# Low parts off GpSimd between the output projection and the early wide products, and kept weight parts at the head of the second half

## The chip, the cores and the metric

The kernel runs on one core of one Trainium2 chip. The metric is device time in microseconds (us). Five engines of the core matter here: TensorE does matrix products and transposes (PE in the profile, with its weight loads as PEld), VectorE (DVE) and ScalarE (ACT) do elementwise work, GpSimd (POOL) does elementwise work too, and SyncE (SP) issues the transfers. Each engine runs its own instructions in the order in which the program issued them, and waits at an instruction until what it reads has been written and the buffer that it writes has come free.

## The reference, cut to what matters

One layer of a hybrid streaming encoder is computed for two groups of tokens, 512 prompt tokens and 32 sample tokens, with a model width of 1024 and shared weights. The change touches the stretch from the output projection to the first products of the feed-forward part:

```python
mix = (g_a * y_a + g_b * y_b) @ w_o
x = layer_norm(ALPHA * x + (1 + g1) * mix, ln1_g, ln1_b)
h2 = layer_norm(x) * (1 + sc2) + sh2
gt, up = jnp.split(h2 @ w_gu, 2, axis=-1)
ffn = (jax.nn.silu(gt) * up) @ w_down
x = layer_norm(ALPHA * x + (1 + g2) * ffn, ln2_g, ln2_b)
```

`h2` therefore needs two layer norms of each token, one behind the other. `w_gu` is 1024 x 5632: 2816 columns for the gate and 2816 for `up`. One small edit lies far earlier, in the differential attention of the sample tokens.

## The kernel before

**Products in two parts.** Every large product is made of three float32r products: a factor is written as a high part (a rounded copy, `hi`, made by ScalarE) and a low part (`lo = raw - hi`), and the result is the sum of hi x hi, hi x low and low x hi. The weights are split while the kernel runs, in pieces of 128 rows x 8 x 128 columns (128x1024 elements). The activations are split too (`h2H`, `h2L` for `h2`).

**Units and the planner.** The kernel is a list of units that `stream` (L1258) walks through. A `Unit` (L1014) of the wide products has 24 matmuls for each half of the tokens (8 slices of the inner dimension, three products each). Half 0 is the tokens 0 to 255; half 1 is the tokens 256 to 511 and the 32 sample tokens, 288 columns. Before a unit runs, `prep` (L1287) has the next unit's weights split; `hi` and `lo` have two buffers each. Everything else (evacuations, norms, softmax) is written as generators that a planner, `Lane` (L467), steps in between the matmuls by its own model of time; its table `LATER` (L34) moves single steps by some microseconds. The planner runs when the program is built, so what it decides is the fixed order of instructions on each engine.

**Output projection.** Eight pieces of `w_o` are split by `split_to` (L2380), and `TokUnit`s accumulate one tile of 128 tokens and 512 columns at a time: first token tiles 0 and 1, then 2, then 3. `tok_end` multiplies by the gate (`z`), adds to `u_t` and takes statistics (`blk_st`).

**Two norms.** `norm_pair(p)` (L2280) starts two `norm_tile`s (L2228), the tiles 2p and 2p+1. A norm tile gets its reciprocal root from GpSimd (`rs`, L722 and L599), applies the norm, gain and bias to `u_t`, takes new statistics, gets a second root and lets ScalarE write `xn`. How gain and bias are applied is set by `MODE` (L2353). With 0 it is two VectorE instructions of 128x1024 (`scalar_tensor_tensor`). With 2, used for tile 2 alone, it is one on ScalarE, one on VectorE and one on GpSimd. Then four `quarter`s (L2288) transpose `xn` on TensorE (`ps_x`), scale and shift it (`h2t`, on ScalarE or VectorE by `ACT_MOD`), and `h2_parts` (L2266) writes `h2H` on ScalarE and `h2L` on VectorE, or on GpSimd for the quarters in `POOL_LO`. Pair 0 and `norm_rows` (the 32 sample tokens) come first; the tiles 2 and 3 feed half 1.

**Early wide products.** The first three column chunks of `w_gu` (`EARLY = 3`) run in halves: twelve units (chunk, column block, gate or up) with half 0, then the same twelve units with half 1, each with its weights split again, in the same order (`order`, L2510). Behind them each chunk runs with both halves. Chunk 0 comes through a ring of two raw buffers, chunks 1 and 2 lie in tiles of their own (`rawg`). The first unit of each half has `need_norm` (L2487): there the planner issues whatever is left of the norms of that half. For each unit, `g_evac` makes `th` from the gate product; `u_evac` (L2472) multiplies it with the `up` product and splits the result into `act` parts, the low part on VectorE, or on GpSimd for the entries of `ACT_POOL`.

**GpSimd's part.** `sub2` (L602) makes a low part in two pieces, 128x384 on GpSimd and 128x640 on VectorE. It is used by `split_to`, so for the pieces of `w_o` and for the splits of the early units.

**Attention.** `attention()` (L1590) begins with a copy of the sample tokens' queries (`q_s`, 128x128, L1594) out of the tile `qka`, on VectorE; the next step, `kH`, writes into the slot that this copy reads.

Of the kernel before, what the change touches and what calls it, by code (L numbers as in the profile page):

```python
# [9 lines left out]
F32 = mybir.dt.float32  # L10
F32R = mybir.dt.float32r
AF = mybir.ActivationFunctionType
# [230 lines left out]
    "norm_pair/1/28": 0.8,  # L243
# [4 lines left out]
    "norm_pair/1/32": -0.5,  # L248
# [11 lines left out]
    "norm_pair/1/5": 5,  # L260
# [14 lines left out]
    "norm_pair/1/9": -1,  # L275
    "norm_rows/0/0": 0.4,
# [6 lines left out]
    "norm_rows/0/8": 3,  # L283
# [3 lines left out]
    "norm_tile/0/5": -1,  # L287
# [94 lines left out]
    "tok_end.g/10/1": 0.4,  # L382
# [13 lines left out]
    "tok_end.g/7/0": 0.4,  # L396
    "tok_end.g/7/2": 0.8,
# [138 lines left out]
def trunk_kernel(ctx: ExitStack, tc: tile.TileContext, I: dict, O: list):  # L536
# [11 lines left out]
    lane = Lane()  # L548
# [24 lines left out]
    def act(out, in_, func, **kw):  # L573
        nc.scalar.activation(out=out, in_=in_, func=func, **kw)  # L574
        lane.op("act", out)
# [18 lines left out]
    def vtt(out, in0, in1, op):  # L594
        nc.vector.tensor_tensor(out=out, in0=in0, in1=in1, op=op)  # L595
        lane.op("dve", out)

    def gtt(out, in0, in1, op):
        nc.gpsimd.tensor_tensor(out=out, in0=in0, in1=in1, op=op)  # L599
# [21 lines left out]
    def vcopy(out, in_):  # L621
        nc.vector.tensor_copy(out=out, in_=in_)
        lane.op("dve", out, 0.8)
# [4 lines left out]
    ADD, SUB, MUL, MAX, MIN = ALU.add, ALU.subtract, ALU.mult, ALU.max, ALU.min  # L628
# [67 lines left out]
    for c in LOADS.split():  # L696
        n = int(c[1:])
# [211 lines left out]
    qk_holder = {}  # L909
# [422 lines left out]
    q_s = s3[:, 1824:1952].rearrange("p (h t) -> p h t", h=4)  # L1332
# [257 lines left out]
    def attention():  # L1590
# [3 lines left out]
        vcopy(q_s, qk_holder["q"][:, :, 512:544])  # L1594
# [463 lines left out]
    units = []  # L2058
# [96 lines left out]
    for br, (W, ev) in enumerate(((I["w_br_a"][0], br_a_evac), (I["w_br_b"][0], br_b_evac))):  # L2155
        for c in range(2):
            src = W[:, c * 512:(c + 1) * 512].rearrange("(k p) c -> p k c", p=128)
            ch = Chunk([(lambda r: r.rearrange("p (k c) -> p k c", k=4), src)])
            for j in range(4):
# [12 lines left out]
                u = Unit(ch, 0, 4, aH, aL, ev(4 * c + j), split=sp_br)  # L2172
# [55 lines left out]
    def norm_tile(tt):  # L2228
# [214 lines left out]
    h2Hk = lambda k: D_["h2H"](k)  # L2443
    h2Lk = lambda k: D_["h2L"](k)
# [42 lines left out]
    def need_norm(hf):  # L2487
        return lambda: lane.until(lambda: hf in norms and all(x[2] for x in norms[hf]))
# [5 lines left out]
    pairs = []  # L2494
    EARLY = 3
# [15 lines left out]
    for c, halves in order:  # L2511
        for j in range(2):
            n = 2 * c + j
            for g, ev in ((0, g_evac), (1, u_evac)):
                u = Unit(
                    pairs[c][g], 128 * j, 8, h2Hk, h2Lk, ev(n), halves=halves,
                    split=gu_split(c, j, g) if c < EARLY else None,
                )
                if (c, j, g) == (0, 0, 0):
                    u.need = need_norm(halves[0])  # L2520
                units.append(u)
        if c == 4:
            units.append(Call(lambda: state.update(gate=lane.add(gate_parts()))))
# [168 lines left out]
```

## Time and profile before

| | us |
|---|---|
| median of 3 runs | 940.01 (938.99 to 941.04) |
| the profiled execution | 941.38 |
| its span | 939.3 |
| TensorE busy | 900.0 (96%) |
| VectorE busy | 522.9 (56%) |
| ScalarE busy | 329.6 (35%) |
| GpSimd busy | 182.5 (19%) |

The span runs from the first to the last instruction of the profiled execution. TensorE is busy for 96% of it, so whole-span shares say little about a change in the order of the other engines: what counts is where TensorE stands still or runs at a lower clock. Of its 39 us of idle time, about 24 lie in the first 25 us and the last 27 us, which the change doesn't touch. The rest is short waits: some 7 us spread over the attention and the stages beside it, and some 8 us gathered between 506 and 546 us, which is the stage of this change. The prediction shows the lines of that stage.

### The profile page before, as it was taken

How to read it: one execution, taken by the hardware profiler on the slowest of the kernel's cores; microseconds unless marked ns; L12 is line 12 of the kernel's file. 1: busy time of each engine (PE TensorE's matmuls, PEld its weight loads, DVE VectorE, ACT ScalarE, POOL GpSimd, SP SyncE). 2: the span in 40 equal slices, each digit the busy share in tenths (PEclk: the TensorE clock that was granted, in tenths of full speed). 3: DMA queues.
4: the chain of work that ended last, by engine and by line, in shares of the span. 5: the costliest groups of instructions: out<-in, count | busy, mean ns of one | idle time of the engine just before them, and what ended most of it. 6: DMA issues, size and time to landing. Idle time of an engine off the chain costs nothing. (4 is left out here: it accounts for less than half of the span.)

```text
span 939.3 us, 16724 instructions
## 1 busy us (share of the span) xinstructions
PE 900.0 (96%) x6903; PEld 824.8 (88%) x6903; DVE 522.9 (56%) x1083; ACT 329.6 (35%) x653; POOL 182.5 (19%) x224
## 2 busy tenths in 40 slices
PE   4999999999999999999998999999999999999995
PEld 3899997988898989999886889999999999777885
DVE  4653559968445444457769865434564455224247
ACT  3343385556532333223403464322232332111110
POOL 3010145433300111103623745100000000000002
PEclk8999999999999999999998999999999999999998
DMA  9924244323343531216806002122332344613202
GB/s 291 342 85 117 83 127 135 102 90 97 132 157 113 185 107 48 95 51 231 263 1 227 32 18 90 47 85 92 126 113 87 124 135 158 238 51 133 90 24 95
DMA packets 89256, 113.05 MB, mean 120 GB/s; under 512 B 4432, under 2 KB 65204, under 8 KB 89180
## 3 DMA queue, kind: packets, MB, share of 16 engines
q1 hardware_dynamic: 88972, 111.92, 36.6%
q8 instruction: 54, 0.88, 0.4%
q14 instruction: 22, 0.18, 0.1%
q10 hardware_dynamic: 208, 0.07, 0.0%
HBM read 104.71 MB, written 7.26 MB: 119 GB/s over the span
## 5 line engine op out<-in xcount | busy, mean ns | idle before, releaser
L595 DVE TENSOR_TENSOR lo<-raw,hi 128x1024 fp32r<-128x1024 f32 (+2 forms) x100 | 113.3, 1133 | 155.3 <-ACT hi L574 154.6
L574 ACT ACTIVATE hi<-raw 128x1024 fp32r<-128x1024 f32 (+1 forms) x116 | 115.7, 997 | 189.5 <-PE dn L1075 78.0
L1043 PE MATMUL g<-h2La,hi 128*128 128x288 f32 (+1 forms) x352 | 102.3, 291 | 2.4 <-DVE h2La L595 1.8
L1043 PE MATMUL g<-h2Ha,lo 128*128 128x288 f32 (+1 forms) x352 | 101.8, 289 | 1.8 <-DVE lo L595 1.5
L1075 PE MATMUL dn<-hi,act 128*128 128x512 f32 (+1 forms) x356 | 103.5, 375 | 0.0
L1043 PE MATMUL g<-h2Hb,hi 128*128 128x288 f32 (+1 forms) x352 | 102.8, 292 | 0.0
L1043 PE MATMUL g<-h2Ha,hi 128*128 128x288 f32 (+1 forms) x352 | 102.3, 291 | 0.1
L1043 PE MATMUL g<-h2Lb,hi 128*128 128x288 f32 (+1 forms) x352 | 102.4, 291 | 0.0
L1043 PE MATMUL g<-h2Hb,lo 128*128 128x288 f32 (+1 forms) x352 | 101.7, 289 | 0.0
L1043 PE MATMUL g<-hHa,hi 128*128 128x256 f32 (+1 forms) x320 | 99.1, 310 | 0.0
L1043 PE MATMUL g<-hHb,hi 128*128 128x256 f32 (+1 forms) x320 | 97.0, 303 | 0.0
L1043 PE MATMUL g<-hLb,hi 128*128 128x256 f32 (+1 forms) x320 | 92.3, 288 | 0.0
L1043 PE MATMUL g<-hLa,hi 128*128 128x256 f32 (+1 forms) x320 | 92.2, 288 | 0.0
L1043 PE MATMUL g<-hHb,lo 128*128 128x256 f32 (+1 forms) x320 | 91.9, 287 | 0.0
L1043 PE MATMUL g<-hHa,lo 128*128 128x256 f32 (+1 forms) x320 | 91.8, 287 | 0.0
L1075 PEld LDWEIGHTS dn<-hi,act 128*128 128x128 f32 x356 | 63.8, 188 | 14.3 <-issue 1.4
L1043 PEld LDWEIGHTS g<-hHa,hi 128*128 128x128 f32 x320 | 60.3, 188 | 12.7 <-issue 7.4
L1043 PEld LDWEIGHTS g<-h2La,hi 128*128 128x128 f32 x352 | 66.6, 189 | 2.9 <-DVE h2La L595 2.0
L1043 PEld LDWEIGHTS g<-h2Ha,lo 128*128 128x128 f32 x352 | 66.8, 190 | 2.5 <-DVE lo L595 1.8
L599 POOL TENSOR_TENSOR lo<-raw,hi 128x1024 fp32r<-128x1024 f32 (+1 forms) x24 | 49.3, 2054 | 97.8 <-ACT hi L574 85.5
L1043 PEld LDWEIGHTS g<-h2Ha,hi 128*128 128x128 f32 x352 | 66.6, 189 | 1.0 <-issue 0.8
L1043 PEld LDWEIGHTS g<-h2Hb,lo 128*128 128x128 f32 x352 | 67.3, 191 | 0.0
(503 smaller groups left out, 2051.9 us busy)
## 6 DMA issues: line engine op xcount, KB each, us to landing
raw<-in_w_gu_dram SPq DMA_DIRECT2D x18, 1024.0 KB, 5.1
raw<-in_w_in_dram SPq DMA_DIRECT2D x12, 1024.0 KB
raw<-in_w_ada_dram SPq DMA_DIRECT2D x12, 1024.0 KB, 5.2
raw<-in_w_down_dram SPq DMA_DIRECT2D x10, 1024.0 KB, 7.7
raw<-in_w_gate_dram SPq DMA_DIRECT2D x8, 1024.0 KB, 7.2
wo<-in_w_o_dram SPq DMA_DIRECT2D x8, 512.0 KB, 7.8
rawg<-in_w_gu_dram SPq DMA_DIRECT2D x4, 1024.0 KB, 5.5
g_part<-in_w_ada_dram SPq DMA_DIRECT2D x16, 256.0 KB, 2.7
```

The costliest lines, as they stand in the source:

```text
L574: nc.scalar.activation(out=out, in_=in_, func=func, **kw)
L595: nc.vector.tensor_tensor(out=out, in0=in0, in1=in1, op=op)
L599: nc.gpsimd.tensor_tensor(out=out, in0=in0, in1=in1, op=op)
L1043: nc.tensor.matmul(ps[:, 0:n], w[:, self.k0 + k, :], a(self.ak0 + k)[:, o:o + n], start=(self.first and k == 0 and p == 0), stop=(self.las ...
L1075: nc.tensor.matmul(a["ps"][:, 0:m.stop - m.start], x(f)[:, 128 * t:128 * t + 128], w[:, k, m], start=first, stop=last)
```

## The change

Six things are done.

1. `sub2` goes; `split_to` makes the whole low part (128x1024) on VectorE. This holds for the eight pieces of `w_o` and all early splits.
2. Token tile 2 is normed like the others, with two VectorE instructions (`MODE`).
3. The two `h2L` quarters of `POOL_LO` and the two `act` low parts of `ACT_POOL` go to VectorE. GpSimd keeps, in this stretch, only the small instructions for the roots.
4. Half 1 of the early units begins with the last two units of half 0 (chunk 2, column block 1, gate and up). These two reuse the `hi` and `lo` that half 0 left in the two buffers, so they have no split. The other ten units follow in their old order.
5. The copy `q_s` in the attention goes from VectorE to ScalarE.
6. `LATER` gets other numbers for steps of `br_b_evac`, `norm_pair`, `norm_rows`, `norm_tile`, `tok_end` and `u_evac`, so the planner puts some steps elsewhere.

```diff
-    def sub2(out, in0, in1, op):
-        gtt(out[:, 0:3], in0[:, 0:3], in1[:, 0:3], op)
-        c = lane.chain
-        lane.begin()
-        vtt(out[:, 3:8], in0[:, 3:8], in1[:, 3:8], op)
-        lane.chain = max(c, lane.chain)
...
-        vcopy(q_s, qk_holder["q"][:, :, 512:544])
+        act(q_s, qk_holder["q"][:, :, 512:544], AF.Copy)
...
-    MODE = ((0, 1), (0, 1), (2, 1), (0, 1))
+    MODE = ((0, 1), (0, 1), (0, 1), (0, 1))
     ACT_MOD = ((0, 2), (0, 1, 3))
-    POOL_LO = ((0, 1), (1, 1))
-    ACT_POOL = ((0, 0), (1, 0))
+    POOL_LO = ()
+    ACT_POOL = ()
...
         act(hi, raw, AF.Copy)
-        sub2(lo, raw, hi.bitcast(F32), SUB)
+        vtt(lo, raw, hi.bitcast(F32), SUB)
...
-    order = [(c, (hf,)) for hf in range(2) for c in range(EARLY)] + [(c, (0, 1)) for c in range(EARLY, 11)]
...
+    early = [(c, j, g) for c in range(EARLY) for j in range(2) for g in range(2)]
+    turn = early[-2:] + early[:-2]
+    order = [(x, (0,)) for x in early] + [(x, (1,)) for x in turn]
+    order += [((c, j, g), (0, 1)) for c in range(EARLY, 11) for j in range(2) for g in range(2)]
+    kept = {}
+
+    def keep(x, halves):
+        c, j, g = x
+        if c >= EARLY:
+            return None
+        if x in kept:
+            return lambda: kept[x].w
+        return gu_split(c, j, g)
+
+    for (c, j, g), halves in order:
+        x = (c, j, g)
+        u = Unit(
+            pairs[c][g], 128 * j, 8, h2Hk, h2Lk, (g_evac, u_evac)[g](2 * c + j), halves=halves, split=keep(x, halves),
+        )
+        if x in turn[:2] and halves == (0,):
+            kept[x] = u
+        if (x, halves) in ((early[0], (0,)), (turn[0], (1,))):
+            u.need = need_norm(halves[0])
+        units.append(u)
```

More of the change, by code (lines that the diff above doesn't have):

```diff
@@ L103 @@
     "br_b_evac.f.g/12/0": 5,
-    "br_b_evac.f.g/12/1": -1,
+    "br_b_evac.f.g/12/1": -0.2,
     "br_b_evac.f.g/13/0": 4.5,
@@ L107 @@
     "br_b_evac.f.g/14/1": 0.8,
+    "br_b_evac.f.g/2/1": -2,
+    "br_b_evac.f.g/3/0": -0.5,
     "br_b_evac.f.g/3/1": -2,
@@ L110 @@
     "br_b_evac.f.g/6/0": -0.6,
-    "br_b_evac.f.g/7/0": -2,
+    "br_b_evac.f.g/7/0": -1.2,
+    "br_b_evac.f.g/7/1": 5,
     "br_b_evac.f.g/8/0": 3,
-    "br_b_evac.f.g/9/0": -1.5,
+    "br_b_evac.f.g/9/0": -1.1,
     "conv_evac.g/1/0": 0.4,
@@ L191 @@
     "norm_pair.quarter/2/2": 0.4,
-    "norm_pair.quarter/2/3": 1.0,
     "norm_pair.quarter/3/1": -0.5,
     "norm_pair.quarter/3/3": -1,
+    "norm_pair.quarter/5/0": -0.5,
     "norm_pair.quarter/5/3": 0.8,
@@ L198 @@
     "norm_pair.quarter/7/0": 1.5,
-    "norm_pair.quarter/7/1": -0.5,
+    "norm_pair.quarter/7/1": -2.5,
     "norm_pair/0/1": 8,
-    "norm_pair/0/10": -0.5,
+    "norm_pair/0/10": 2.5,
     "norm_pair/0/11": -1.5,
@@ L212 @@
     "norm_pair/0/28": 4.2,
-    "norm_pair/0/29": 10,
+    "norm_pair/0/29": 11.5,
     "norm_pair/0/3": 1.6,
     "norm_pair/0/32": -2,
-    "norm_pair/0/34": 1.2,
+    "norm_pair/0/34": 1.6,
     "norm_pair/0/35": -0.5,
@@ L219 @@
     "norm_pair/0/37": 5,
+    "norm_pair/0/38": -0.5,
     "norm_pair/0/39": 4.0,
@@ L229 @@
     "norm_pair/0/8": -0.5,
-    "norm_pair/1/1": 0.8,
+    "norm_pair/1/1": 2.3,
     "norm_pair/1/10": -1.2,
+    "norm_pair/1/11": 5,
     "norm_pair/1/13": -1.2,
@@ L242 @@
     "norm_pair/1/27": 0.8,
-    "norm_pair/1/28": 0.8,
+    "norm_pair/1/28": -0.2,
     "norm_pair/1/29": 5.4,
@@ L247 @@
     "norm_pair/1/31": 3,
-    "norm_pair/1/32": -0.5,
+    "norm_pair/1/32": 2.5,
     "norm_pair/1/36": -1,
@@ L259 @@
     "norm_pair/1/48": -1,
-    "norm_pair/1/5": 5,
+    "norm_pair/1/5": 8,
     "norm_pair/1/50": -0.2,
@@ L274 @@
     "norm_pair/1/71": 5,
-    "norm_pair/1/9": -1,
-    "norm_rows/0/0": 0.4,
     "norm_rows/0/1": -0.5,
@@ L282 @@
     "norm_rows/0/6": -2.5,
-    "norm_rows/0/8": 3,
     "norm_rows/0/9": -2,
@@ L286 @@
     "norm_tile/0/1": 1.5,
-    "norm_tile/0/5": -1,
+    "norm_tile/1/0": 3,
     "norm_tile/1/1": -1,
@@ L291 @@
     "norm_tile/2/0": -2.2,
+    "norm_tile/2/1": -2,
     "norm_tile/2/2": 0.3,
     "norm_tile/2/3": 3,
-    "norm_tile/2/4": -1.5,
+    "norm_tile/2/4": -0.7,
     "norm_tile/2/5": -2,
     "norm_tile/3/0": 0.8,
-    "norm_tile/3/1": 2.3,
     "q_split/0/0": -2,
@@ L381 @@
     "tok_end.g/10/0": 1.5,
-    "tok_end.g/10/1": 0.4,
     "tok_end.g/10/2": -0.2,
@@ L386 @@
     "tok_end.g/13/2": -0.5,
-    "tok_end.g/2/0": 3,
     "tok_end.g/2/1": -1.6,
+    "tok_end.g/2/2": 0.8,
     "tok_end.g/3/0": -0.8,
@@ L396 @@
     "tok_end.g/7/0": 0.4,
+    "tok_end.g/7/1": -0.5,
     "tok_end.g/7/2": 0.8,
@@ L401 @@
     "tok_end.g/9/2": -0.5,
+    "u_evac.f.g/0/0": -2,
     "u_evac.f.g/0/1": -1,
     "u_evac.f.g/1/1": 0.8,
+    "u_evac.f.g/10/0": -2,
     "u_evac.f.g/10/1": 0.5,
@@ L409 @@
     "u_evac.f.g/14/0": 5,
-    "u_evac.f.g/14/1": 1.9,
+    "u_evac.f.g/14/1": 2.7,
+    "u_evac.f.g/15/0": -2,
     "u_evac.f.g/15/1": 6.5,
     "u_evac.f.g/16/0": 1.5,
-    "u_evac.f.g/16/1": 3,
-    "u_evac.f.g/17/1": -2,
+    "u_evac.f.g/17/1": -2.5,
     "u_evac.f.g/18/0": -0.5,
-    "u_evac.f.g/19/0": -0.2,
+    "u_evac.f.g/19/0": 0.2,
     "u_evac.f.g/19/1": 1.5,
@@ L2508, in gu_split @@
         return lambda: split_to(raw(), None)
-    order = [(c, (hf,)) for hf in range(2) for c in range(EARLY)] + [(c, (0, 1)) for c in range(EARLY, 11)]
[L2511 to L2521, printed above, removed]
+    early = [(c, j, g) for c in range(EARLY) for j in range(2) for g in range(2)]
[20 more added lines that the diff above has]
+        units.append(u)
+        if (j, g) != (1, 1):
+            continue
         if c == 4:
```

## The prediction

> **What bounds the kernel now.** I read the busy time by stage first: the stretch before the output projection ends, then the early wide products of half 0 (506 to 558.65 us, where the first product of half 1 starts), then all that follows. The columns are the window, its length, busy time and instructions of PE, PEld, DVE, ACT and POOL, the mean granted clock, the share of the DMA engines and GB/s. The last row is the first product of half 1 in the timeline.
>
> ```profile
> 506.00:558.65 52.65, 44.53 (x326) 42.53 (x325) 41.00 (x67) 28.29 (x45) 30.31 (x29) 0.90 0.27 93
> 558.65:912.00 353.35, 353.35 (x2686) 328.15 (x2685) 159.54 (x242) 97.52 (x164) 17.56 (x11) 1.00 0.32 106
> ```
>
> ```profile
> 558.65 0.29 PE L1043 MATMUL g<-h2Ha,hi 128*128 128x288 f32 x1
> ```
>
> After 558.65 TensorE never stops until 912 us, at full clock: nothing that the change does to side engines there can gain. In the stage itself TensorE is idle for 52.65 - 44.53 = 8.12 us and its mean granted clock is 0.90. The waits of TensorE from 440 to 600 us, in total with the longest, say at what:
>
> ```profile
> PE ps_x L584 <- ACT xn L574: 2.3, 1, 2.3
> PE g L1043 <- DVE h2La L595: 1.8, 1, 1.8
> PE g L1043 <- DVE lo L595: 1.5, 1, 1.5
> PE ps_x L584 <- DVE h2t L591: 0.8, 1, 0.8
> PE g L1043 <- POOL h2La L599: 0.7, 1, 0.7
> PE ps_x L584 <- ACT h2t L574: 0.7, 1, 0.7
> ```
>
> Four of them (4.0 us) stand at the start of half 0, two (3.8 us) at its end, behind a weight low part and behind `xn` of the second norm pair. The waits are not the whole loss. The windows by 5 us show what follows each group, with two short ones for the pace:
>
> ```profile
> 510.00:515.00 5.00, 2.46 (x11) 1.89 (x10) 4.92 (x10) 1.76 (x4) 2.76 (x3) 0.66 1.08 354
> 515.00:520.00 5.00, 5.00 (x30) 5.00 (x31) 1.54 (x3) 1.30 (x2) 0.00 (x0) 0.65 0.41 130
> 545.00:550.00 5.00, 4.37 (x24) 4.38 (x25) 0.60 (x2) 3.51 (x8) 0.25 (x1) 0.66 0.00 0
> 547.00:549.00 2.00, 2.00 (x11) 2.00 (x10) 0.00 (x0) 1.53 (x4) 0.00 (x0) 0.50 0.00 0
> 551.00:553.00 2.00, 2.00 (x20) 2.00 (x19) 2.00 (x3) 1.15 (x3) 0.83 (x1) 1.00 0.00 0
> ```
>
> The granted clock falls to 0.50, and 11 matmuls pass in 2 us instead of 20. With a floor of 0.50, a mean of 0.66 over 5 us is 3.4 us of half clock, so about 6.9 us at the first place and 3.4 us at the second. At half clock a busy microsecond does half a microsecond's work: the first place loses about (6.9 - 1.4 idle) / 2 = 2.7 us, the second 3.4 / 2 = 1.7 us. The stage's loss is 8.1 + 4.4 = 12.5 us.
>
> The chain that ended last, in order of time, says which engine is behind the second group (start, length, what):
>
> ```profile
> 536.91 2.07 POOL u_t L599
> 538.98 1.55 POOL lo L599
> ...
> 544.33 1.25 ACT xn L574
> 545.63 1.03 PE ps_x L584 x4
> ```
>
> Ahead of `xn` stands GpSimd, with the bias of tile 2 and a weight low part; between the rows shown come the two roots of the norm pair (the rows left out), queued behind them on that engine.
>
> **The change part by part.**
>
> **GpSimd slows VectorE, so its work costs VectorE little.** Instructions of one kind, from the timeline of VectorE:
>
> ```profile
> 526.15 0.82 DVE L595 TENSOR_TENSOR lo<-rawg,hi 128x640 fp32r<-128x640 f32 x1 [0.53 <-ACT hi L574]
> 537.40 2.26 DVE L595 TENSOR_TENSOR lo<-rawg,hi 128x640 fp32r<-128x640 f32 x1
> 488.44 1.28 DVE L618 SCALAR_TENSOR_TENSOR u_t<-u_t,mv__5730,s_u 128x1024 f32<-128x1024 f32 x1
> 511.65 0.69 DVE L595 TENSOR_TENSOR h2La<-h2t,h2Ha 128x512 fp32r<-128x512 f32 x1
> ```
>
> The same 128x640 low part takes 0.82 us alone and 2.26 us beside GpSimd's `u_t` of the chain above (536.91 us). It is the very one for which TensorE waits 1.5 us. So I add up VectorE's stage anew, from its groups between 506 and 558.65 us and, for the full-width low part, from 600 to 700 us:
>
> ```profile
> L595 DVE TENSOR_TENSOR lo<-rawg,hi 128x640 fp32r<-128x640 f32 x8 | 9.4, 1169 | 1.2 <-ACT hi L574 1.1
> L595 DVE TENSOR_TENSOR lo<-raw,hi 128x640 fp32r<-128x640 f32 x4 | 4.5, 1113 | 0.5 <-ACT hi L574 0.5
> L595 DVE TENSOR_TENSOR h2Lb<-h2t,h2Hb 128x512 fp32r<-128x512 f32 x3 | 3.1, 1051 | 0.0
> L595 DVE TENSOR_TENSOR h2La<-h2t,h2Ha 128x512 fp32r<-128x512 f32 x2 | 2.2, 1095 | 0.0
> L595 DVE TENSOR_TENSOR h2La<-h2t,h2Ha 128x128 fp32r<-128x128 f32 x1 | 1.1, 1097 | 0.0
> L595 DVE TENSOR_TENSOR act<-th,act 128x256 fp32r<-128x256 f32 x2 | 0.8, 422 | 2.4 <-ACT act L574 2.4
> ```
>
> ```profile
> L595 DVE TENSOR_TENSOR lo<-raw,hi 128x1024 fp32r<-128x1024 f32 x16 | 19.6, 1225 | 8.3 <-ACT hi L574 8.3
> ```
>
> - Low parts of weights: twelve now, 9.4 + 4.5 = 13.9 us. The twelfth belongs to the first unit of half 1, which keeps its parts: eleven of 1.225 us, 13.5 us. Change -0.4.
> - `h2L` quarters: five at 5.3 us become seven at 0.69 us, 4.8 us. Change -0.5. The small 128x128 one falls from 1.1 to about 0.3 us (estimate: a quarter of the 0.69 row and a fixed part). Change -0.8.
> - Two more `act` low parts at 0.42 us. Change +0.8.
> - Tile 2: I take four instructions of 1.28 us for both tiles, 5.1 us, against 2.0 + 1.6 us for tile 3 and 1.2 us for tile 2's one. Change +0.3.
>
> Together -0.6 us: VectorE stays at about 40.4 us. GpSimd's 30.3 us fall to the roots, and ScalarE's 28.3 us lose 1.2 us (tile 2) and two `hi`. Latencies shorten: a weight low part ends one 1.23 us instruction behind its `hi` instead of behind GpSimd, and a root no longer queues behind a low part like that of 1.55 us in the chain.
>
> [...]
>
> **The end of half 0.** If everything falls into place, 1.5 + 2.3 us of waits and 1.7 us of half clock go: 5.5 us. **The start of half 0**: the second `h2La` quarter follows the first on VectorE at 0.69 us instead of ending on GpSimd at 514.7, so 0.7 us of wait goes. The other three waits hang on a VectorE that is full from 510 to 515 us (4.92 of 5); the wider low parts there (two, +0.4 us each) and the end of GpSimd's interference about cancel, and I count nothing.
>
> **Bound by VectorE.** VectorE now idles 52.65 - 41.00 = 11.65 us in the stage. Two of these waits belong to the stall itself:
>
> ```profile
> 545.91 0.43 DVE L595 TENSOR_TENSOR act<-th,act 128x256 fp32r<-128x256 f32 x1 [2.39 <-ACT act L574]
> 549.83 0.42 DVE L618 SCALAR_TENSOR_TENSOR th<-th,g 128x256 f32<-128x256 f32 x1 [3.49 <-ACT th L574]
> ```
>
> Without these 5.9 us, 5.8 us of dependent waits stay: 40.4 + 5.8 = 46.2 us, 6.4 us less than now, which is close to TensorE's 5.5 + 0.7 = 6.2. The two engines then finish together, with nothing spare, so some low part will be late: of gains from 0 (VectorE's new work falls in the wrong order) to 6.4 I take two thirds, **4.3 us**. Kept parts help just there: in the last two units of half 0 no weights are split, which leaves VectorE and ScalarE to `h2` of half 1.
>
> **The copy in the attention.** The rows of the three engines and TensorE's longest wait there:
>
> ```profile
> 106.31 2.39 POOL L599 TENSOR_TENSOR lo<-raw,hi 128x1024 fp32r<-128x1024 f32 x1 [10.08 <-ACT hi L574]
> 107.22 2.05 DVE L622 COPY s_att<-qka 128x128 f32<-128x128 f32 x1
> 109.31 1.15 ACT L574 ACTIVATE kH<-qkb 128x512 fp32r<-128x512 f32 x2 [3.08 <-DVE s_att L622]
> ```
>
> ```profile
> PE s_ps L1683 <- DVE kL L595: 1.2, 1, 1.2
> ```
>
> The copy takes 2.05 us beside a GpSimd instruction; `kH` waits for it, `kL` for `kH`, and TensorE 1.2 us for `kL`. ScalarE has been idle for 3.08 us then, so it can copy about 2 us earlier, and the wait goes. What is queued behind the copy on ScalarE is `kH` itself, which had to wait for it anyway. Bounds: 1.2 us gained, or nothing if the planner, whose times shift a little, orders the attention worse. I take 1.0.
>
> **What is hidden.** The wider low parts of `w_o` lie under a TensorE that has no wait between 440 and 506 us in the list above. The ring buffers of chunk 0 are released two units later in half 1: twelve matmul-bound units stand there, and loads of this kind land in some 5 us:
>
> ```profile
> raw<-in_w_gu_dram SPq DMA_DIRECT2D x18, 1024.0 KB, 5.1
> ```
>
> Six units of 24 matmuls remain before chunk 3 is split. At 0.1 us a matmul (20 in 2 us) or more, that is over 14 us against two loads; nothing waits. If that cover failed, TensorE would stand for a load, 5 us. The first `x1d` stores and the queue of SP don't move against these loads by more than the planner's shifts.
>
> **Sum.** -4.3 - 1.0 = -5.3 us. The profiled execution took 941.38 us (span 939.3), 1.4 us above the median of 940.01; from it the forecast is 936.1, and at the median **934.7 us**.
>
> **The rivals.**
> - **All goes.** The half-clock stretch at the start of half 0 also shrinks from 6.9 to 3.4 us (-1.7), since TensorE's first 3.4 us there are no longer broken by the 0.7 us wait. With 6.4 and 1.2 that is -9.3: 930.7 us. For it: two gains have the same cause. Against: VectorE would have to be on time everywhere.
> - **The stall moves, nothing is won.** The planner, which now counts more VectorE work, puts weight low parts first and the norms of tiles 2 and 3 later; TensorE waits as long as now, behind VectorE instead of GpSimd. Only the copy gains: 939.0 us, and 938.1 to 941.9 is what I call the same. For it: VectorE would be 40.4 us busy of some 46.
> - **VectorE becomes the bound, slower.** The last steps of the second norm pair slip to the `need_norm` at the head of half 1, where nothing covers them. The price is that of the first pair, which starts uncovered today: 4.0 us of waits, 2.7 us of half clock, and 2.3 us for `xn` ahead of it, 9.0 us in place of 2.3 + 1.7. That is +5.0; with the 0.7 and 1.0 us saved, 943.3 us. It decides when the second statistics of the pair, now ended at 541.1 us and 17.5 us ahead of half 1, come within some 6 us of it. Against it: kept parts free 2.5 us of VectorE (two low parts) just before. The row of those statistics:
>
> ```profile
> 540.89 0.21 DVE L614 BATCH_NORM_AGGREGATE mv__6204<-st__6201 128x2 f32<-128x12 f32 x1
> ```
>
> [...]
>
> **How the numbers follow.** Forecast (4 to 8 us less scatter, 932 to 938.1) 0.58; all goes, 0.10; nothing won 0.17; slower 0.15. A measurement of this kernel tells about 0.2% (1.9 us) from no change. So faster 0.68, the same 0.17, slower 0.15. The range reaches from the rival at 930.7 to just over the band of no change: 931 to 942 us.
>
> **What would show it.** Right: GpSimd at about 7 us in the stage; 128x1024 low parts at 1.2 us throughout; no wait for `xn` and no clock below 1.00 between 540 and 555 us; `kH` starting near 107 us; half 1 starting four to six us sooner. Wrong: waits for `lo`, `h2L` or `xn` in the stage that add up to 4 us again, a half-clock stretch at the head of half 1, or new waits in the attention.

## The result, and the profile after

| | before | after |
|---|---|---|
| median of 7 runs, us | 940.06 (938.99 to 943.54) | 933.29 (931.2 to 935.78) |
| the profiled execution, us | 941.38 | 931.58 |
| its span, us | 939.3 | 929.9 |

The ratio is 0.9923, with a 95% interval from 0.991 to 0.9935. The kernel is 6.8 us faster at the medians; the forecast was 5.3 us. The two profiled executions lie 9.8 us apart, but 2.9 of these are not the change's: from the start to the first transpose of `v_tok` (where the changed attention begins) one execution took 93.62 us and the other 90.75 us, with the same instructions. The granted clock was 0.50 there for 10.2 us in the one (16.7 to 26.9 us) and for 3.4 us in the other (19.5 to 22.9 us); TensorE was busy for 1.3 us longer in the one (79.77 against 78.45 us) and stood still for 1.6 us longer. So I go by stretches, each from one instruction of TensorE to another.

The windows view of the kernel after, with the same columns as in the prediction. The first row is the stage, from the first transpose of `xn` for half 0 to the first product of half 1; then the attention's stretch from `v_tok` to the first product of `mo_ps`, with its first part, up to the first product with `kL`; then the 5 us at each of the two places that the prediction named, and all that follows.

```profile
501.64:549.15 47.51, 42.59 (x325) 40.85 (x324) 39.62 (x71) 25.82 (x43) 7.05 (x12) 0.93 0.30 102
90.75:284.44 193.69, 189.25 (x1502) 169.20 (x1501) 128.93 (x321) 104.47 (x263) 62.19 (x70) 1.00 0.37 118
90.75:107.19 16.44, 16.44 (x133) 15.98 (x133) 9.35 (x22) 5.66 (x13) 3.19 (x4) 1.00 0.37 126
505.00:510.00 5.00, 2.91 (x14) 2.39 (x14) 4.87 (x10) 2.17 (x5) 0.00 (x0) 0.76 1.08 352
510.00:515.00 5.00, 5.00 (x28) 5.00 (x27) 3.42 (x12) 1.52 (x3) 0.00 (x0) 0.56 0.50 158
540.00:545.00 5.00, 4.83 (x41) 4.63 (x40) 4.11 (x6) 4.90 (x8) 0.00 (x0) 1.00 0.00 0
545.00:550.00 5.00, 5.00 (x44) 5.00 (x43) 3.22 (x8) 3.05 (x7) 0.00 (x0) 1.00 0.00 0
549.15:905.00 355.85, 355.85 (x2698) 330.24 (x2697) 159.37 (x242) 96.42 (x163) 0.00 (x0) 1.00 0.32 105
```

The stage and the attention's two windows of the kernel before:

```profile
506.26:558.65 52.39, 44.27 (x325) 42.39 (x324) 40.74 (x67) 28.29 (x45) 30.31 (x29) 0.90 0.27 92
93.62:288.96 195.34, 189.56 (x1502) 169.31 (x1500) 130.17 (x322) 103.97 (x262) 62.17 (x70) 1.00 0.37 117
93.62:111.84 18.22, 17.00 (x136) 16.33 (x135) 10.65 (x23) 5.35 (x12) 3.18 (x4) 1.00 0.34 113
```

The stage is 52.39 - 47.51 = 4.9 us shorter. TensorE's idle time in it falls from 52.39 - 44.27 = 8.12 to 47.51 - 42.59 = 4.92 us, which is 3.2 us. The rest is the clock: 6.8 us at half clock remain (0.76 and 0.56 at the start of half 0), and the 3.4 us at its end are gone, so a busy TensorE does the same work in 1.7 us less. The attention's stretch is 195.34 - 193.69 = 1.7 us shorter, and in its first part TensorE has no idle time any more (1.22 us before). That part alone shrinks by 1.8 us, but it also has three matmuls fewer (133 for 136), which now run behind it, so the longer stretch is the fair one. 1.7 + 4.9 = 6.6 us, close to the 6.8 of the medians. Behind half 1's first product both kernels run alike: it is 380.7 us to the end in both.

TensorE's waits from 495 to 560 us after the change (what waited, what it waited for, us in total, times, longest):

```profile
PE g L1040 <- DVE h2La L599: 1.5, 2, 0.8
PE g L1040 <- DVE lo L599: 1.1, 2, 0.9
PE ps_x L588 <- ACT h2t L578: 0.7, 1, 0.7
PE ps_x L588 <- ACT xn L578: 0.6, 1, 0.6
PE g L1040 <- ACT h2Ha L578: 0.6, 1, 0.6
PE ps_x L588 <- DVE h2t L595: 0.4, 1, 0.4
```

The longest wait is 0.9 us where it was 2.3. The wait for GpSimd's `h2La` is gone, but 0.8 us for VectorE's `h2La` stand at the same place. At the end of half 0, `lo` costs 0.9 (and 0.2) instead of 1.5 us, and `xn` 0.6 instead of 2.3.

VectorE by groups in the stage (count, total us, mean ns, idle time before them), four of its groups, and what is left of GpSimd there at the end of half 0, in the timeline:

```profile
L599 DVE TENSOR_TENSOR lo<-rawg,hi 128x1024 fp32r<-128x1024 f32 x8 | 9.8, 1223 | 1.6 <-ACT hi L578 1.6
L599 DVE TENSOR_TENSOR h2La<-h2t,h2Ha 128x512 fp32r<-128x512 f32 x4 | 2.7, 684 | 0.0
L599 DVE TENSOR_TENSOR h2Lb<-h2t,h2Hb 128x512 fp32r<-128x512 f32 x3 | 2.0, 683 | 0.7 <-ACT h2Hb L578 0.7
L599 DVE TENSOR_TENSOR act<-th,act 128x256 fp32r<-128x256 f32 x5 | 2.0, 420 | 0.0
```

```profile
533.53 0.19 POOL L719 TENSOR_SCALAR rs__6222<-mv__6176 128x1 f32<-128x1 f32 x1 [11.04 <-DVE mv__6176 L611]
...
536.32 0.19 POOL L719 TENSOR_SCALAR rs__6243<-mv__6205 128x1 f32<-128x1 f32 x1 [0.75 <-DVE mv__6205 L611]
536.59 1.47 POOL L603 TENSOR_TENSOR rs__6243<-rs__6243,nhalf 128x1 f32<-128x1 f32 x1
538.16 0.29 POOL L776 TENSOR_SCALAR nb__6244<-mv__6205,rs__6243 128x1 f32<-128x1 f32 x1
```

The reader is to see two things. Every `h2L` quarter takes 0.68 us where the two groups before took 1.05 and 1.10. And the first instruction of a root now waits for VectorE's statistics (`mv`) and for nothing else: GpSimd had been idle for 11 us.

### The profile page after: what moved, and what is told of

The parts are those of the page before. It is cut to its first block, busy times and chain, and to the rows that moved or that the text cites. A ratio compares the mean times of both kernels' runs of the same rounds, so it can differ in the third digit from the quotient of the medians.

```text
span 929.9 us, 16633 instructions
## 1 busy us (share of the span) xinstructions
PE 896.6 (96%) x6903; PEld 822.2 (88%) x6903; DVE 519.9 (56%) x1085; ACT 326.3 (35%) x651; POOL 125.4 (13%) x186
## 4 chain that ended last, share of the span: by engine, by line
PE 54%; DVE 4%; POOL 1%; issue 0%; ACT 0%; POOLq 0%; DVEq 0%
PE g L1040 35%; PE dn L1072 12%; PE wo L1072 5%; PE dn L1102 1%; DVE lo L599 1%; DVE blk_st L607 0%; DVE y_ta L615 0%; PE wo L1102 0%; DVE z L599 0%; DVE y_tb L615 0%; PE mo_ps L582 0%; DVE u_t L615 0%; PE ps_x L588 0%; ACT hi L578 0%; DVE h2t L595 0%
## 5 line engine op out<-in xcount | busy, mean ns | idle before, releaser
L599 DVE TENSOR_TENSOR lo<-raw,hi 128x1024 fp32r<-128x1024 f32 (+1 forms) x100 | 114.6, 1146 | 158.2 <-ACT hi L578 157.5
L1040 PEld LDWEIGHTS g<-h2Lb,hi 128*128 128x128 f32 x352 | 66.7, 190 | 0.0
```

Of the source, the lines that this page charges most:

```text
L1040: nc.tensor.matmul(ps[:, 0:n], w[:, self.k0 + k, :], a(self.ak0 + k)[:, o:o + n], start=(self.first and k == 0 and p == 0), stop=(self.las ...
```

## The experiments

In the table, "stage" is the window from the first transpose of `xn` to the first product of half 1 in each kernel's own profile, "idle" what TensorE stands still in it, and "half clock" the number of stretches of 3.4 us at a granted clock of 0.50. The ratio stands against the kernel before, run beside it on the same chip.

| kernel | ratio (95% interval) | median, us | stage | idle | half clock |
|---|---|---|---|---|---|
| before | 1 | 940.06 | 52.39 | 8.12 | 3 |
| after | 0.9923 (0.991 to 0.9935) | 933.29 | 47.51 | 4.92 | 2 |
| e1_copy | 0.9977 (0.9966 to 0.9988) | 938.6 | 53.93 | 9.02 | 4 |
| e2_swap | 0.9964 (0.995 to 0.9977) | 936.52 | 48.55 | 6.87 | 1 |
| e3_two_pieces | 0.9916 (0.9898 to 0.9934) | 932.82 | 46.69 | 4.72 | 1 |
| e4_resplit | 0.9916 (0.99 to 0.9933) | 932.88 | 47.34 | 4.90 | 2 |
| e5_tile2 | 0.9995 (0.9986 to 1.0005) | 940.54 | 53.02 | 8.31 | 3 |
| e6_old_table | 0.9912 (0.9898 to 0.9927) | 932.83 | 48.26 | 5.23 | 2 |
| e7_all_back | 0.9962 (0.9947 to 0.9976) | 936.54 | 50.05 | 6.37 | 2 |
| e8_start | 0.9898 (0.9882 to 0.9915) | 931.05 | 45.44 | 5.46 | 0 |
| e9_no_add | 0.992 (0.9901 to 0.994) | 933.21 | 47.58 | 4.32 | 2 |
| e10_add_only | 0.9937 (0.9917 to 0.9957) | 934.21 | 47.67 | 5.17 | 2 |
| e11_start_again | 0.991 (0.989 to 0.993) | 932.93 | 45.43 | 5.48 | 0 |
| e12_after_again | 0.9928 (0.9913 to 0.9942) | 933.46 | 47.55 | 4.95 | 2 |

The theory was the prediction's: GpSimd's work slows VectorE (a low part of 128x640 takes 0.82 us alone and 2.26 us beside GpSimd's `u_t`), so it costs VectorE next to nothing to take it over, and the end of half 0 stops waiting. The expectations call it the theory of the port; the runs show by how much instructions grow, not by what. Its rivals here were that the new order (the planner's table, the kept parts) does it, and that one single instruction of GpSimd, the long bias add of tile 2, does it.

### The copy alone

The kernel before with the one edit:

```diff
-        vcopy(q_s, qk_holder["q"][:, :, 512:544])
+        act(q_s, qk_holder["q"][:, :, 512:544], AF.Copy)
```

> The kernel before with one edit: the copy q_s on ScalarE. From the first v_tok transpose to the first s_ps product with kL the profiles show 18.22 us before and 16.44 us after the change. If the copy alone makes this (my theory), that stretch is 16.4 to 16.7 us, the rest stands as before (first product of half 0 to first product of half 1 at 48.4 us), and the time is 1.2 to 1.8 us below the kernel before. If the gain came from something else, or is given back later in the attention, the time is within 0.5 us of before.

Measured: 0.9977, about 2 us. The same two windows of the attention in this kernel:

```profile
91.28:284.91 193.63, 189.26 (x1501) 169.19 (x1500) 128.60 (x321) 104.47 (x263) 62.27 (x70) 1.00 0.36 118
91.28:107.71 16.43, 16.43 (x133) 15.97 (x133) 9.35 (x22) 5.66 (x13) 3.19 (x4) 1.00 0.36 123
```

195.34 became 193.63 us, as in the kernel after, while the stage kept its waits. (Its 9.02 us of idle time are 0.9 more than before, most of it in one wait for GpSimd's `h2La` of 1.5 us that was 0.7 before, though no edit touched it.) So the copy is worth 1.7 us by itself, and the rest of the change nothing in the attention.

ScalarE's timeline in the kernel after shows how:

```profile
103.27 0.30 ACT L578 ACTIVATE s_att<-qka 128x128 f32<-128x128 f32 x1
103.60 1.15 ACT L578 ACTIVATE kH<-qkb 128x512 fp32r<-128x512 f32 x2
```

The copy (`s_att<-qka`) takes 0.30 us on ScalarE where it took 2.05 us on VectorE. Counted from the first transpose of `v_tok`, it begins 1.1 us earlier than before, and `kH` 2.8 us earlier.

### The engine alone

The kernel before, with every instruction at its place in every engine's order, but the pieces that GpSimd made in the stretch issued on VectorE. `lane.op` is the planner's own count; it is told the old engines, so that it plans as before.

```diff
     def sub2(out, in0, in1, op):
-        gtt(out[:, 0:3], in0[:, 0:3], in1[:, 0:3], op)
+        nc.vector.tensor_tensor(out=out, in0=in0, in1=in1, op=op)
+        lane.op("pool", out[:, 0:3])
         c = lane.chain
         lane.begin()
-        vtt(out[:, 3:8], in0[:, 3:8], in1[:, 3:8], op)
+        lane.op("dve", out[:, 3:8])
...
+    def on_dve(out, in0, in1, op):
+        nc.vector.tensor_tensor(out=out, in0=in0, in1=in1, op=op)
+        lane.op("pool", out)
...
-            (vtt if MODE[tt][0] == 1 else gtt)(u, u, D_["b"], ADD)
+            (vtt if MODE[tt][0] == 1 else on_dve)(u, u, D_["b"], ADD)
...
-        (gtt if i in POOL_LO else vtt)(L, tf, H.bitcast(F32), SUB)
+        (on_dve if i in POOL_LO else vtt)(L, tf, H.bitcast(F32), SUB)
...
-                (gtt if (n, hf) in ACT_POOL else vtt)(dL[:, 0:256], th[:, 0:256], dH[:, 0:256].bitcast(F32), SUB)
+                (on_dve if (n, hf) in ACT_POOL else vtt)(dL[:, 0:256], th[:, 0:256], dH[:, 0:256].bitcast(F32), SUB)
```

> The kernel before, its order of instructions kept on every engine, with only the engine changed: what GpSimd made between the output projection and the early products (parts of weights, two h2L quarters, two act low parts, the bias of tile 2) is made by VectorE at the same places; the planner's model is told the old engines. No kept parts, no new table. Theory of the port (GpSimd's work costs VectorE as much as doing it itself): VectorE's busy time in the stage stays within 1.5 us of 41.0 us, and the stage from the first product of half 0 to that of half 1 falls from 48.4 us by 2 to 5 us. Theory of the kept parts, or of the table: the stage stays at 48.4 us or grows, since neither is in. Theory of a VectorE at its bound: the stage grows by 2 us or more.

The stage of this kernel in the windows view, and two of its waits of TensorE:

```profile
505.11:553.66 48.55, 41.68 (x325) 40.03 (x324) 40.55 (x72) 27.87 (x45) 9.53 (x13) 0.96 0.29 99
```

```profile
PE g L1048 <- DVE lo L603: 2.6, 3, 1.0
...
PE ps_x L584 <- ACT xn L574: 1.3, 1, 1.3
```

GpSimd falls from 30.3 to 9.5 us, and VectorE, which took over those pieces, is busy for 40.55 instead of 40.74 us. That is the plainest answer to the prediction's first step: twenty microseconds of GpSimd's work cost VectorE nothing. The kernel is faster by 0.36% (3.4 us of 940). But its waits at the end of half 0 haven't gone: 2.6 us in three places for `lo` (the longest 1.0) and 1.3 for `xn` are 3.9 us, against 1.5 + 2.3 before. They are only spread, so that none is longer than 1.3 us. TensorE's idle time falls by 1.25 us in all, most of it at the start of half 0, and its busy time by 44.27 - 41.68 = 2.6 us, as this profile has one stretch of half clock instead of three. So in this profile the swap alone gains more by the clock than by the waits. That the waits stay because the order of VectorE's work was made for two engines is likely, but not shown here.

### Single parts of the change undone

Three kernels are the kernel after with one part back. In e3_two_pieces the low parts of weights are made in two pieces again, 128x384 on GpSimd and 128x640 on VectorE, with the order of the kernel after:

```diff
-        vtt(lo, raw, hi.bitcast(F32), SUB)
+        h = hi.bitcast(F32)
+        nc.gpsimd.tensor_tensor(out=lo[:, 0:3], in0=raw[:, 0:3], in1=h[:, 0:3], op=SUB)
+        nc.vector.tensor_tensor(out=lo[:, 3:8], in0=raw[:, 3:8], in1=h[:, 3:8], op=SUB)
+        lane.op("dve", lo)
```

> The kernel after, its order kept, with the weight low parts in two pieces again (128x384 on GpSimd, 128x640 on VectorE); all else as after. Theory of the port: the VectorE pieces take 1.1 us on the mean, not 0.82 us, roots queue behind GpSimd's pieces, and the stage grows from 43.5 us by 1.5 to 4 us. Theory that kept parts or the table carry the gain: the stage stays within 1 us of 43.5 us.

In e4_resplit the two kept units have their parts made again, without the planner knowing of it:

```diff
         if x in kept:
-            return lambda: kept[x].w
+            def again():
+                raw = pairs[c][g].raw.rearrange("p (k c) -> p k c", c=256)[:, :, 128 * j:128 * j + 128]
+                hi, lo = part_pair(None)
+                nc.scalar.activation(out=hi, in_=raw, func=AF.Copy)
+                nc.vector.tensor_tensor(out=lo, in0=raw, in1=hi.bitcast(F32), op=SUB)
+                return hi, lo
+            return again
```

> The kernel after, its order kept, but the two units at the head of half 1 split their weights again (two more high parts on ScalarE, two more low parts on VectorE; the planner isn't told). Theory of the port: kept parts give slack only, the stage grows by 0 to 1.5 us. Theory of the kept parts: the second norm pair's work comes 2.5 us late at the head of half 1, TensorE waits there and the half clock returns, and the stage grows by 2.5 to 5 us.

In e6_old_table `LATER` has the numbers of the kernel before (37 entries differ; two of them are shown):

```diff
-    "norm_pair/1/1": 2.3,
+    "norm_pair/1/1": 0.8,
...
-    "norm_tile/2/1": -2,
```

> The kernel after with the planner's table of the kernel before: engines, kept parts and the early copy as after, the order other. Theory that the engines and a planner that knows them make the gain: idle in the stage stays at 4.5 to 6 us and the time within 1.5 us of after. Theory that the new table carries the last 2 us: idle is 6.5 to 8.5 us and the time 2 to 4 us above after.

None of the three lost anything that can be measured: 0.9916, 0.9916 and 0.9912. For e3_two_pieces I had expected 1.5 to 4 us of growth, and this was wrong, although the interference is there. Its stage, and the VectorE half of its low parts:

```profile
503.77:550.46 46.69, 41.97 (x325) 39.66 (x324) 40.64 (x71) 25.84 (x43) 19.38 (x22) 0.96 0.31 104
```

```profile
L2382 DVE TENSOR_TENSOR lo<-rawg,hi 128x640 fp32r<-128x640 f32 x8 | 8.2, 1030 | 1.1 <-ACT hi L578 1.1
```

VectorE is busy for 40.64 us against 39.62, though it handles 640 of 1024 columns: a piece takes 1.03 us on the mean, 0.82 alone. So GpSimd's pieces buy nothing, but no long wait of TensorE depends on them in this order. The kept parts aren't needed either: with them made again the stage has the same length, and the stretch behind it, from half 1 to the down projection, takes 233.24 instead of 232.56 us, 0.7 us more in one profile. The table is worth nothing that can be measured.

### Tile 2's add alone, in the old order

The kernel before, in which only the add of tile 2's bias (128x1024) goes to VectorE:

```diff
-            (vtt if MODE[tt][0] == 1 else gtt)(u, u, D_["b"], ADD)
+            (vtt if MODE[tt][0] == 1 else on_dve)(u, u, D_["b"], ADD)
```

> The kernel before, its order kept, with one instruction moved: the bias add of tile 2 (2.39 us on GpSimd) is made by VectorE at the same place. TensorE's idle time from the first transpose of xn to the first product of half 1 was 8.1 us before, 6.9 us with all of GpSimd's pieces moved, and 4.9 us after. If this one instruction (in the chain, and beside the low part of 2.26 us) carries the swap's gain, idle falls to 6 to 7 us and the time by 1 to 3 us. If the many small pieces do, idle stays at 7.5 to 8.5 us and the time within 1 us of before.

Measured: 0.9995, no change. The wait for `lo` fell from 1.5 to 0.6 us, but the one for `xn` rose from 2.3 to 2.7. GpSimd's timeline in this kernel, the statistics on VectorE and the transposes on TensorE show why:

```profile
537.55 1.89 POOL L599 TENSOR_TENSOR lo<-rawg,hi 128x384 fp32r<-128x384 f32 x1 [1.70 <-ACT hi L574]
539.53 0.19 POOL L726 TENSOR_SCALAR rs__6221<-mv__6160 128x1 f32<-128x1 f32 x1
539.80 0.55 POOL L599 TENSOR_TENSOR rs__6221<-rs__6221,nhalf 128x1 f32<-128x1 f32 x1
540.46 1.08 POOL L783 TENSOR_SCALAR nb__6222<-mv__6160,rs__6221 128x1 f32<-128x1 f32 x1
541.62 0.19 POOL L726 TENSOR_SCALAR rs__6242<-mv__6204 128x1 f32<-128x1 f32 x1
```

```profile
539.92 0.21 DVE L618 BATCH_NORM_AGGREGATE mv__6204<-st__6201 128x2 f32<-128x12 f32 x1
```

```profile
544.66 0.84 PE L584 MATMUL ps_x<-ident,xn 128*128 128x128 f32 x4 [2.71 <-ACT xn L574]
```

The second tile's statistics are ready at 540.13 us, but its root begins at 541.62, behind the root of the other tile, which itself stood behind a weight piece of 1.89 us. So, as far as the timeline shows, with one long instruction of the engine gone, the next in the same queue sets the end.

### All of GpSimd's pieces back in the new order, and its two halves

In e7_all_back all pieces that GpSimd lost are given back to it in the kernel after (tile 2's first multiplication then is ScalarE's, as before), with the order of the kernel after. The weight pieces are those of e3_two_pieces; the others:

```diff
-            stt(u, u, rs, D_["b"], MUL, ADD)
+            if tt == 2:
+                nc.scalar.activation(out=u, in_=u, func=AF.Identity, scale=rs)
+                nc.gpsimd.tensor_tensor(out=u, in0=u, in1=D_["b"], op=ADD)
+                lane.op("dve", u)
+            else:
+                stt(u, u, rs, D_["b"], MUL, ADD)
...
-        (gtt if i in POOL_LO else vtt)(L, tf, H.bitcast(F32), SUB)
+        if i in ((0, 1), (1, 1)):
+            nc.gpsimd.tensor_tensor(out=L, in0=tf, in1=H.bitcast(F32), op=SUB)
+            lane.op("dve", L)
+        else:
+            vtt(L, tf, H.bitcast(F32), SUB)
...
-                (gtt if (n, hf) in ACT_POOL else vtt)(dL[:, 0:256], th[:, 0:256], dH[:, 0:256].bitcast(F32), SUB)
+                if (n, hf) in ((0, 0), (1, 0)):
+                    nc.gpsimd.tensor_tensor(out=dL[:, 0:256], in0=th[:, 0:256], in1=dH[:, 0:256].bitcast(F32), op=SUB)
+                    lane.op("dve", dL[:, 0:256])
+                else:
+                    vtt(dL[:, 0:256], th[:, 0:256], dH[:, 0:256].bitcast(F32), SUB)
```

> The kernel after, its order kept, with all of GpSimd's pieces back at their places: weight low parts in two pieces, two h2L quarters, two act low parts, tile 2's bias add (with ScalarE multiplying by the root). Low parts in two pieces alone cost nothing in this order. Theory of the port and of the chain through GpSimd: idle grows from 4.9 to 6.5 us or more and the time by 2 us or more. Theory that the order alone makes the gain: idle stays at 4.5 to 5.5 us.

Measured: 0.9962, about half of the gain lost. GpSimd's timeline and the product that waits for it:

```profile
528.52 1.72 POOL L2493 TENSOR_TENSOR act<-th,act 128x256 fp32r<-128x256 f32 x1
530.20 2.96 POOL L2246 TENSOR_TENSOR u_t<-u_t,s_u 128x1024 f32<-128x1024 f32 x1
533.13 2.54 POOL L2390 TENSOR_TENSOR lo<-rawg,hi 128x384 fp32r<-128x384 f32 x2
```

```profile
534.75 0.39 PE L1040 MATMUL g<-h2Ha,lo 128*128 128x256 f32 x1 [3.03 <-POOL lo L2390]
```

From 528.52 to 534.75 us GpSimd has no gap: an `act` piece, the long add, and behind them the weight piece for which TensorE stands still for 3.03 us. From 531 to 534 us the granted clock was 1.00, from 536 to 539 us 0.50.

The next two kernels take this apart. e9_no_add is e7_all_back without the first block of that diff, so tile 2 stays on VectorE; e10_add_only has that block alone.

> The order of after with GpSimd's pieces back except tile 2's bias add: weight low parts in two pieces, two h2L quarters, two act low parts. With the add as well, idle in the stage was 6.4 us with one wait of 3.0 us for a weight piece queued on GpSimd behind an act low part and the add. Theory of the queue (the long add ahead of a weight piece makes the wait): the 3.0 us wait is gone, idle is 4.5 to 5.5 us and the time within 1.5 us of after. Theory of the sum of small pieces: idle stays over 6 us.

> The order of after with tile 2's bias add alone on GpSimd (ScalarE multiplies by the root); weight low parts stay whole on VectorE. Theory of the queue: nothing that TensorE needs is queued behind the add, so no wait of 3 us; idle 4.5 to 5.5 us. Theory of the port: the VectorE instruction beside the add takes 2.3 us or more instead of 1.2 us, a weight low part or the second statistics come 1 to 2 us late, and idle is 5.5 to 7 us.

e9_no_add is as fast as the kernel after within the intervals, 0.992, with GpSimd busy for 24.76 us of its stage; the wait of 3.0 us is gone and the idle time is 4.32 us, as the theory of the queue had it. e10_add_only lies between, 0.9937, with an interval that reaches to both sides; its idle time of 5.17 us is less than the 5.5 us that the theory of the port asked for, but the slowed instruction of that theory is there. What its add does is seen in the timelines of GpSimd, VectorE and TensorE:

```profile
527.20 2.40 POOL L2246 TENSOR_TENSOR u_t<-u_t,s_u 128x1024 f32<-128x1024 f32 x1 [5.09 <-ACT u_t L2245]
```

```profile
527.26 2.62 DVE L599 TENSOR_TENSOR act<-th,act 128x256 fp32r<-128x256 f32 x1
529.81 1.27 DVE L615 SCALAR_TENSOR_TENSOR u_t<-u_t,rs__6072,s_u 128x1024 f32<-128x1024 f32 x1
531.01 0.41 DVE L599 TENSOR_TENSOR th<-th,g 128x256 f32<-128x256 f32 x1
531.34 1.21 DVE L599 TENSOR_TENSOR lo<-rawg,hi 128x1024 fp32r<-128x1024 f32 x1
```

```profile
532.60 0.39 PE L1040 MATMUL g<-h2Ha,lo 128*128 128x256 f32 x1 [1.94 <-DVE lo L599]
```

The add takes 2.40 us, and an `act` low part of VectorE that takes 0.42 us elsewhere takes 2.62 us beside it. That is 2.2 us lost. VectorE saves one `u_t` instruction of 1.28 us in return, which ScalarE and GpSimd do, so the weight low part behind comes about 1.0 us later than in the kernel after (counted from the statistics `mv__6040`, some 11 us ahead of it on VectorE), and TensorE waits for 1.94 instead of 0.94 us. The same add hurts in two ways: it holds VectorE up, and it holds up what stands behind it on GpSimd. Without it all other pieces together cost nothing that can be measured in this order.

### The start of half 0

The kernel after with five numbers of the table changed: three steps of `tok_end` and one of a `quarter` come later, and one step of another `quarter` earlier, so that VectorE makes `h2La` sooner. e11_start_again repeats it and e12_after_again the kernel after, side by side and with more executions.

```diff
 LATER = {
+    "tok_end.g/6/2": 3,
+    "norm_pair.quarter/2/3": 3,
...
-    "norm_pair.quarter/1/2": 0.4,
+    "norm_pair.quarter/1/2": -1,
...
-    "tok_end.g/7/1": -0.5,
-    "tok_end.g/7/2": 0.8,
+    "tok_end.g/7/1": 2,
+    "tok_end.g/7/2": 3,
```

> The kernel after with five numbers of the planner's table changed, so that at the start of half 0 VectorE makes both h2La quarters ahead of the adds and statistics of tiles 2 and 3. TensorE waits there 0.7 and 0.8 us for h2La. If VectorE's order is what holds the start, idle falls from 4.9 to 3.2 to 4 us and the time by 1 to 2 us. If tiles 2 and 3 then come late at the head of half 1, idle and time stay or grow.

> The kernel with the five other numbers in the table (VectorE makes both h2La quarters first), once more, beside after on the same chip: 0.5 to 2.5 us below after if its first result was no chance of the half-clock windows; within 0.5 us of after otherwise.

> The kernel after itself, once more, as the neighbour of the run above and to see how the number of half-clock windows in the stage varies for one kernel: 932 to 934.5 us, idle in the stage at 4.9 us within 0.3 us, one to three windows of 3.4 us.

The stage of e8_start, with 6 us at its beginning:

```profile
501.30:546.74 45.44, 39.98 (x326) 38.12 (x325) 39.37 (x71) 25.94 (x43) 6.94 (x12) 1.00 0.31 106
503.00:509.00 6.00, 3.51 (x23) 2.70 (x23) 5.19 (x11) 3.09 (x6) 0.74 (x2) 1.00 1.07 353
```

I had expected less idle time, and there is more: 5.46 us against 4.92. One wait for `h2La` went, and waits for `xns` and `h2Lb` of 0.7 and 0.6 us came. But the clock stays at 1.00 through the whole stage, and the stage is 2.1 us shorter. Both profiles of this kernel show it, both of the kernel after show two half-clock stretches. The whole time is less clear: 931.05 us, and 932.93 against 933.46 us side by side, with intervals that overlap. What the traces show of the clock there stands in the last section. This version is not slower than the kernel after, and how much faster it is stays open between nothing and about 2 us.

## Why the prediction was right

**Sign, place and size.** Counted from the start of the stage, half 1 begins 4.9 us sooner where "four to six" was forecast, and the attention gives the rest. 6.8 us came at the medians where 5.3 were forecast; the time lies inside the range, 1.4 us below the forecast. The stage's 4.3 us were two thirds of 6.4, and no row gave that factor, so that it came near 4.9 is in part luck. The waits for `lo`, `h2L` and `xn` add up to 1.1 + 1.5 + 0.6 = 3.2 us, not far from the 4 us that were to show the prediction wrong.

**GpSimd's work costs VectorE nothing: right, and shown** by e2_swap (40.55 against 40.74 us with all of it taken over). Item by item: whole low parts 1.22 us (1.225 in the sum), seven `h2L` at 0.68 (0.69), `act` low parts 0.42 (0.42). In the same window VectorE lost 1.1 us where 0.6 was forecast.

**The end of half 0: right in size, less simple in cause.** Of 1.5 + 2.3 + 1.7 us, 0.6 + 1.7 + 1.7 = 4.0 went (0.9 of the wait for `lo` and 0.6 for `xn` stay, so "no wait for `xn`" was too strong). The clock stays at 1.00 from 540 to 550 us, as forecast. The prediction named tile 2's add and the weight piece behind it, on one queue ahead of the roots. In the new order that add is indeed what makes the other pieces hurt (e7_all_back against e9_no_add, 3.3 us at the medians); the pieces without it cost nothing, and what the add costs alone is unclear (e10_add_only). In the old order it isn't enough to take the add away (e5_tile2, nothing): its timeline shows the roots behind the weight piece. The old order with the pieces gone and the add kept wasn't run, so how the 3.4 us of e2_swap divide between them stays open.

The prediction also put the end of these waits down to the engine. That was too simple: for weight parts and `xn` together TensorE waits at the end of half 0 for 3.8 us before and still 3.9 with the engine alone (e2_swap), for 2.2 in the new order with the old table (e6_old_table) and 1.7 after. In the order of the kernel after it is 4.0 us with all of GpSimd's pieces back, but 1.5 with the small pieces alone (e9_no_add) and 1.9 with the add alone (e10_add_only). These are single profiles, but they agree: the waits go with the new order, and come back in it only when the pieces and the add are both on GpSimd.

**What the order is worth.** With the copy's 0.9977 taken out, the change's stage is 0.9923 / 0.9977 = 0.9946, some 5.1 us. The engine alone in the old order gave 0.9964, 3.4 us; giving everything back in the new order lost 0.9962 / 0.9923, 3.7 us. Both ways some 1.5 us are left for the new order, with an uncertainty as large as itself. Neither the table (e6_old_table) nor the kept parts (e4_resplit) show a share of it. It may be that the planner now counts VectorE's work where it really is; the order of units at the head of half 1 wasn't tried alone. This stays open.

**"Kept parts help just there": wrong.** This was the reason given for VectorE to be on time. Making the parts again left the stage at 47.34 against 47.51 us, and cost 0.7 us behind it in one profile.

**The start of half 0: right in the sum, one term wrong.** I counted 0.7 us for GpSimd's `h2La`. That wait went, but 0.8 us for VectorE's came in its place. The waits there still fell from 3.9 us (the prediction's 4.0 without rounding) to 3.2, the 0.7 that was forecast, but by other terms, which had been counted as nothing: 0.4 us less for one `h2t`, and the first wait for `h2La` (1.8 us) turned into 0.6 for `h2Ha` and 0.7 for `h2La`. That the sum fits is luck. The half clock there stayed as forecast, 6.8 us (6.9 before). The rival "all goes" wanted it to shrink. In e8_start it is gone (1.00 through the stage), by another way than the one I gave; that unbroken work in the first 3.4 us would shorten it, no run here shows.

**The copy: the mechanism right, its size too small.** 1.0 us was taken with 1.2 as the upper bound; e1_copy shows 1.7. The wait for `kL` went, and with it TensorE's idle time in the attention fell from 195.34 - 189.56 = 5.78 to 193.69 - 189.25 = 4.44 us, 1.3 us. The other 0.3 us lie in TensorE's busy time over the same matmuls (189.56 and 189.25 us); what shortens it isn't shown. The bound of 1.2 us held the wait alone, and the 1.0 took a loss to the planner's shifts that didn't come.

**The rivals.** "VectorE becomes the bound" gave waits of 9 us at the head of half 1; there is none, and the longest wait behind VectorE is 0.9 us. "The stall moves" didn't happen in the kernel after: TensorE waited for VectorE for 4.1 us in this stage before (`h2La`, `lo` and `h2t`) and waits for 3.0 us now, and only the 0.8 us for the second `h2La` have moved over from GpSimd.

## What to carry to other kernels

Before you give an engine small pieces of work to use its idle time, look at the longest instruction in its queue: what counted here was what stood behind it and what it did to the other engine's instructions beside it (e7_all_back, with the add of 2.96 us, is 3.3 us slower than e9_no_add), not the sum of busy times. Have the order planned anew for the engines that do the work. Moving such work back to the busier engine was free here (20.8 us of GpSimd's, and VectorE busy for 40.55 instead of 40.74 us), and two rows of one instruction, alone and beside the other engine (0.82 and 2.26 us), had told this ahead of time. When one culprit is taken away and the time doesn't move, follow the next instruction in the same queue before you give the theory up.

## What was not expected of the hardware

**Half clock came in stretches of 3.4 us.** In the traces of the kernels before and after, the granted clock was 0.50 for 10.24, 6.82 and 3.41 us in the one and for 3.41 and 6.82 us in the other (three, two and one times 3.41 us), and once more at the end of the program, behind TensorE's last product. In the stages of the other twelve the mean clock fits none to four stretches of 3.4 us (e1_copy: 0.87 over 53.93 us is 14.0 us at 0.50). At the end of half 0 a stretch followed a wait of TensorE of 1.94 (e10_add_only), 2.3 (before), 2.7 (e5_tile2) and 3.03 us (e7_all_back), and none followed one of 0.94 (after), 1.3 (e2_swap) or 1.5 us (before, for `lo`). At the start of half 0, no wait is longer than 0.8 us, and the clock falls all the same in the kernel after; in e8_start, with 5.46 us of short waits in the stage, it doesn't.

**The longest wait alone didn't tell where the clock fell.** Several short waits close together were followed by half clock as well as a long one. In the 3.41 us ahead of a stretch in the stage, TensorE was busy for 1.53 (start of half 0) and 1.09 us (its end) in the kernel before, and for 1.83 us (start of half 0) in the kernel after. Two windows of e10_add_only, in its wait of 1.94 us and behind it:

```profile
530.00:533.00 3.00, 1.06 (x9) 0.85 (x8) 3.00 (x4) 1.64 (x3) 0.00 (x0) 1.00 0.37 147
534.00:536.00 2.00, 2.00 (x12) 2.00 (x11) 2.00 (x4) 0.00 (x0) 1.74 (x3) 0.50 0.27 102
```

But in e8_start TensorE stood still for 6.00 - 3.51 = 2.49 us of the 6 us from 503 us, at 1.00 (its window stands with the experiment), and in e2_swap for 1.32 us of the 5 us from 540 us, and the clock stayed at 1.00 for the 10 us from there. How much idle time in how short a time is enough, and what else decides, these traces don't show.

**Such stretches also came and went between executions** at places that no edit touched: at the start of the kernel 3.4 us in the profile of the kernel after, 10.2 us in the one before. What one costs can be read in the stage, where one less went with 1.7 us less of TensorE's busy time (44.27 and 42.59 us). So two single profiles can't be compared by their spans.

**A short instruction of GpSimd varied by a factor of three.** One instruction of a root, with 128x1, took 0.55 us twice and 1.40, 1.47 and 1.58 us in the stage of the kernel after. Two of them in GpSimd's timeline:

```profile
520.00 0.55 POOL L603 TENSOR_TENSOR rs__6031<-rs__6031,nhalf 128x1 f32<-128x1 f32 x1
520.91 1.58 POOL L603 TENSOR_TENSOR rs__6072<-rs__6072,nhalf 128x1 f32<-128x1 f32 x1
```

VectorE made a weight low part from 520.86 to 522.08 us, beside the longer one; but it was at work for a part of the shorter one too (a `th` from 519.91 to 520.33 us). What makes the one longer isn't shown.
